# Weights split into a rounded part and a remainder: by two GpSimd DMAs instead of a staging load and a VectorE subtraction

## The chip, the cores and the metric

One core of a Trainium2 chip runs the whole program. The metric is device time in microseconds, from launch to end, as the median of several executions. The engines are TensorE (PE in the profile, with its weight loads as PEld), VectorE (DVE), ScalarE (ACT), GpSimd (POOL) and SyncE (SP, which here only issues DMAs).

## The reference

A two-layer encoder over 512 tokens of width 1024, all in float32. Each layer is a mixer (layer 0: grouped attention and a bidirectional mLSTM; layer 1: neighbourhood attention and differential attention), then cross-attention into 256 memory tokens, then a gated MLP of width 2816 with a convolution over positions. For the change only the matrix products with weights matter:

```python
for l in range(DEPTH):
    h = rms_norm(x, norm_mix[l])
    x = x + mixer(h)                       # h @ w_in ... @ w_out
    x = x + memory_cross_attention(...)    # h @ w_q, m @ w_kv, ... @ w_o
    x = x + conv_ffn(...)                  # h @ w_up, conv, silu(gate) * val, @ w_down
```

## The kernel before

Each product with weights is made in three TensorE passes, so that it comes out near float32. A weight tile W is split into hi, which is W rounded to fp32r (the format in which TensorE takes a 4-byte number at full rate), and lo = W - hi. The activations are split in the same way by earlier code. `mm3` then adds W_hi H_hi, W_hi H_lo and W_lo H_hi in one PSUM bank. So a full weight tile, 128 rows by 1024 columns (512 KB), feeds 8 x 3 = 24 matmuls of 512 columns.

Where a weight tile comes from: `stage` (line 460) loads it from HBM with a DMA on SP's queue into a buffer of class "st". `weights` (line 466) takes a buffer of class "w" (hi in its first 1024 columns, lo in the other 1024) and calls `split` (line 436): a copy with rounding, on ScalarE or VectorE, and then a VectorE subtraction. There are 246 such tiles: 88 for the MLP's up projection, 48 for its down projection (in threes of 1024, 1024 and 768 columns), 24 for the odd mixer's input, 22 for the even mixer's, 32 of 512 columns for the mixers' outputs, 16 for the memory's keys and values, 16 for the query and output projections of cross-attention. One of them, `w1`, is staged by hand at the start of the program.

The order is not the program's text order. `Recorder` records all instructions, `schedule` (line 237) runs a list schedule over them with planned costs (`cost`, line 167), and `trace` emits each engine's instructions in the order that results. On the chip an engine keeps that order and waits in it. Only the order is fixed by the plan, not the times. A buffer of a class is taken at its first write and given back after its last use; the tags boost some instructions, those of weights by 60 places. Of the planned costs these matter here: a matmul is its columns / 2400 + 0.0027; ScalarE needs 0.09 + 0.000835 per column; a step from one engine to another adds `LAT` = 0.13; and of DMAs

```python
            return (0.06 if eng == "sync" else 1.0), 0.0      # line 179: time on the issuing queue
...
                    if e == "gpsimd":
                        end = now + 3.2                       # line 340: planned landing
```

Buffers: 4 of class "st" and 3 of class "w". GpSimd has only 32 `affine_select` (masks of the mLSTM's decay matrices) and some memsets. All recorded instructions are emitted at line 391, so the profile shows them as L391; they are told apart by tile names: st, w, a (activations), p (PSUM), c (columns of statistics), ident.

Of the kernel before, what the change touches and what calls it, by code (L numbers as in the profile page):

```python
# [11 lines left out]
F32 = mybir.dt.float32  # L12
F32R = mybir.dt.float32r
AF = mybir.ActivationFunctionType
OP = mybir.AluOpType
# [7 lines left out]
LN_EXP_SET = 6  # L23
SILU_SET = 18

SLOTS = {"a": (80, 512), "st": (4, 1024), "w": (3, 2048), "c": (48, 8), "p": (8, 512)}

ROWS = "p (i c) -> p i c"
COLS = "p (c i) -> p i c"
# [22 lines left out]


class Buf:
    """A buffer of one slot class; the slot is chosen when the schedule is made."""

    def __init__(self, cls, ap=None):
        self.cls, self.ap = cls, ap
# [1 line left out]


class View:
    """A recorded view of a Buf; resolved to an access pattern when its instruction is traced."""

    def __init__(self, buf, ops, dummy):
        self.buf, self.ops, self.dummy = buf, ops, dummy
# [19 lines left out]
        return View(self.buf, self.ops + (("to_broadcast", shape),), np.broadcast_to(np.int8(0), shape))  # L86

    def grid(self, pattern, i):
        """[p, n] as [p, i, n/i] ("p (i c) -> p i c") or, of columns in the other order, "p (c i) -> p i c"."""
        p, n = self.dummy.shape  # L90
        return View(self.buf, self.ops + (("grid", (pattern, i)),), np.broadcast_to(np.int8(0), (p, i, n // i)))

    def spread(self, n):
        """[p, m] as [p, m, n], each element n times."""
        p, m = self.dummy.shape
        return View(self.buf, self.ops + (("spread", n),), np.broadcast_to(np.int8(0), (p, m, n)))

# [14 lines left out]


class Op:
    """An instruction: alts holds (engine, method, args, keywords, cost, latency) for each engine that may run it."""

    __slots__ = ("idx", "alts", "pick", "preds", "succs", "need", "bufs", "allocs", "end", "placed", "prio", "boost")

# [16 lines left out]


class Recorder:
    """Records instructions with their buffers, orders them by a list schedule, then traces them in that order."""

    LAT = 0.13  # L140

# [93 lines left out]
        return op  # L235

    def schedule(self, slots):
        """List schedule: each engine takes, of the instructions that are ready, the first in program order. A
        buffer is given one of its class's slots with its first write and gives it back after its last use."""
        import heapq  # L240
        n_ops = len(self.ops)
        free = {c: [(0.0, i) for i in range(n)] for c, n in slots.items()}
        room = {c: np.full(n_ops + 1, n) for c, n in slots.items()}
        first, last = {}, {}
# [149 lines left out]
class Kern:  # L394
# [50 lines left out]
            self.nc.scaled(out, src, gain[rows])  # L445

    def rest(self, lo, src, hi, gain=None, rows=slice(None)):
        """lo: what scaled_copy's rounding left of src * gain."""
        if gain is None:
            self.nc.vector.tensor_tensor(lo, src, hi.bitcast(F32), op=OP.subtract)  # L450
        else:
            self.nc.vector.scalar_tensor_tensor(lo, src, gain[rows], hi.bitcast(F32), op0=OP.mult, op1=OP.subtract)
# [11 lines left out]
        return st, w  # L464

    def weights(self, src):
        nc = self.nc
        st, w = src if isinstance(src, tuple) else self.stage(src)
        wb = self._new("w", 2048, F32R)
        wh, wl = wb[:, :1024], wb[:, 1024:]  # L470
        with self.nc.boosted("w"):
            self.split(wh[:, :w], wl[:, :w], st[:, :w])
        return wh, wl

    def gemm(self, out, src, hs, first=True, last=True):
# [35 lines left out]
class Norm:  # L511
# [27 lines left out]
            nc.vector.tensor_tensor(self.acc, self.acc, sq, op=OP.add)  # L539

    def columns(self):
        """rstd, and its square, of token 128 * t + p in row p of columns t and 4 + t."""
        K, nt = self.K, self.n // 128
        nc = K.nc
        p = K.ps("t")[:, :32 * nt]
        for t in range(nt):
            nc.tensor.transpose(p[:, 32 * t:32 * t + 32], self.r[0:32, t * 128:t * 128 + 128], K.ident[0:32, 0:32])
        self.rc = K.col("rc")
        nc.vector.tensor_copy(self.rc[:, :nt].grid(ROWS, nt), p.grid(ROWS, nt)[:, :, 0:1])
        nc.vector.tensor_tensor(self.rc[:, 4:4 + nt], self.rc[:, :nt], self.rc[:, :nt], op=OP.mult)  # L550
# [14 lines left out]


def softmax(K, sc, n, bias=None):
    """exp(sc - max) and 1 / its sum, of sc and of a bias added to it."""
    nc = K.nc
    c = K.col("sm")  # L570
    P = K.a("P")[:, :n]
    if bias is None:
        nc.vector.tensor_reduce(c[:, 0:1], sc, op=OP.max, axis=AX.X, negate=True)
        nc.scalar.activation(P, sc, AF.Exp, bias=c[:, 0:1], accum_out=c[:, 1:2])
    else:
        nc.vector.tensor_tensor_reduce(P, sc, bias, -1.0, 3.0e38, op0=OP.add, op1=OP.min, accum_out=c[:, 0:1])
        nc.scalar.activation(P, P, AF.Exp, bias=c[:, 0:1], scale=-1.0, accum_out=c[:, 1:2])
    nc.vector.reciprocal(c[:, 2:3], c[:, 1:2])
    return P, c[:, 2:3]


class Head:
    """One head, or two (parts) of 64 columns each: score(i, part) -> P of query tile i, finish(Ps) -> P tiles by part,
    v(kt) -> the stationary operands of key block kt by part, take(y)."""

    def __init__(self, score, v, take, finish=None, plan=None, col=None, nkt=4, parts=1):
        self.score, self.v, self.take, self.parts = score, v, take, parts
# [67 lines left out]


def merge(main, fill, name, rest=True):
    """Emit main, with fill's work spread through it (ratio of PE time), and then what is left of fill (rest)."""
    debt, ratio = TUNE[name + "0"], TUNE[name]
    for c in main:  # L660
        debt += c * ratio
        while fill is not None and debt > 0:
            try:
                debt -= next(fill)
            except StopIteration:
                fill = None
        yield c
    if rest and fill is not None:
        yield from fill
# [10 lines left out]


def q_stack(K, q, gain=None):
    """Two heads' [hi; lo] rows: [qa_hi; qa_lo] and [qb_lo; qb_hi]."""
    lo, hi = slice(0, 64), slice(64, 128)
    qa, qb = K.ar("qa"), K.ar("qb")
    for t, src, dst in ((qa, lo, hi), (qb, hi, lo)):
        K.scaled_copy(t[src], q[src], gain, src)
        K.rest(t[dst], q[src], t[src], gain, src)
    return qa, qb


def k_stack(K, k, gain=None):
    """What the stacked q is multiplied with, of two heads: hi against both its halves, lo against its hi half."""
    nc = K.nc
    halves = slice(0, 64), slice(64, 128)
    out = []
    for i, src in enumerate(halves):
        kh, kl = K.ar("kh"), K.ar("kl")
        for dst in halves:
            K.scaled_copy(kh[dst], k[src], gain, src)  # L700
        nc.gpsimd.memset(kl[halves[1 - i]].bitcast(F32), 0.0)
        K.rest(kl[src], k[src], kh[src], gain, src)
        out.append((kh, kl))
    return out


def scores2(K, q2, k2, i, keys=None):
    """Query tile i against all keys, or against two key tiles."""
    nc = K.nc
    p = K.ps("s")  # L710
    c = slice(i * 128, i * 128 + 128)
# [12 lines left out]
def trunk(ctx, tc, xT, memT, vec, lam_in, rope, ev_w, ev_o, od_w, od_o, ca_q, ca_kv, ca_o, up, down, na_u, t5, outT):  # L724
# [19 lines left out]
    nc = K.nc  # L744
# [45 lines left out]
        return t  # L790

    def tok_gemm(w, nrm, width):
        """Token rows times `width` columns of a matrix: a bank holds 512 // width blocks of 128 tokens."""
        kp, per = 1024 // width, 512 // width
        banks = [K.ps("g") for _ in range(nrm.n // (128 * per))]
        chunks = KT // kp
# [14 lines left out]
        return banks  # L811

    class Tok:
        """Token rows: groups of `width` columns, each a list of banks."""

        def __init__(self, width):
            self.width, self.groups = width, []
# [4 lines left out]
            return self.groups[g][b], j * self.width + o  # L822

    def tok_values(w, nrm, v, roll=False):
        """Values, each token row times its rstd; roll: row n goes to row n + 64."""
        width, per = v.width, 512 // v.width
        banks = yield from tok_gemm(w, nrm, width)
        out = [K.a("v") for _ in banks]
# [11 lines left out]
        v.groups.append(out)  # L840

    def tok_norm(w, nrm, width, refine):
        """Token rows, rms_norm over each head of 64, but for its gain. A list of transposed 128-column chunks."""
        per, nh = 512 // width, width // 64
        banks = yield from tok_gemm(w, nrm, width)
        xs = []
# [21 lines left out]
        return xs  # L868

    def tok_heads(w, nrm, width, gain, refine, stack, roll=False):  # L870
        """Heads of 64 with their gain, transposed and stacked; roll: token n goes to column n + 64."""
        per = 512 // width
        xs = yield from tok_norm(w, nrm, width, refine)
        out = []
# [18 lines left out]
        return t  # L893

    def proj_norm(w, m, nrm, ones, gain, n=S, d=64, refine=False):
        """rms_norm over each head of (h * nrm.r) @ w: scale free but for eps, which becomes eps / nrm.r ** 2.
        refine: a Newton step on the root, which turns its sign; gain is negated for it."""
        p = K.ps("g")[:, :n]
        yield from K.gemm(p, w[m], nrm.hs)
        with nc.boosted("qk"):  # L900
            return norm_bank(p, nrm, ones, gain, n, d, refine)
# [277 lines left out]
        yield from odd_proj(nrm, st, 12, TOK["na"], gcol("naq"), vcol("nak"), True)  # L1179

    def na(st, ys):
        """A tile of 128 tokens is 16 grid columns. Keys are turned by 8 columns, so that the windows of query tile i
        lie in key tiles i and i + 1; the last tile's follows on the first, whose halves are at the grid's two ends."""
        def pair(j):
            def score(i, half):
                b = K.a("u")[:, :256]
# [18 lines left out]
    mems = []  # L1205

    def mem_norm(l):
        """The memory times a layer's gain; its rstd is the same for both layers."""
        nm = Norm(K, vcol("mem", 8 * l, 8), 256)
        for k in range(KT):  # L1210
            t = K.a("mem")[:, :256]
# [243 lines left out]


def _rows(yT):
    """The output's columns are tokens in column-major order of the grid."""
    return np.ascontiguousarray(yT.reshape(D, 64, 8).transpose(2, 1, 0)).reshape(1, S, D)


# [13 lines left out]
```

## Time and profile before

| | |
|---|---|
| device time, 3 runs | 1449.54, 1453.91, 1457.04 us |
| median | 1453.91 us |
| span of the profiled execution | 1447.9 us |
| median less that span | 6.0 us |
| TensorE busy | 1430.4 us, 99% of the span |
| VectorE, ScalarE, GpSimd busy | 966.4, 760.4, 24.0 us |
| moved by DMA | 135.70 MB |

The span runs from the first to the last instruction of the profiled execution. The time of that execution by the device's own measure is not listed apart, so the median is put beside the span: 1453.91 - 1447.9 = 6.0 us lie around it. Matmuls are pipelined, so the mean duration of one (390 ns) is longer than the distance from one to the next (about 230 ns).

### The profile page before, as it was taken

What the parts mean: (1) busy time and instruction counts of PE and PEld (TensorE: products, weight loads), DVE (VectorE), ACT (ScalarE), POOL (GpSimd) and SP (SyncE); (2) the same over time, 40 slices, a digit from 0 to 9 for tenths busy, and PEclk for the clock granted to TensorE, in tenths of its full rate; (3) what the DMA queues carried; (4) which work ended last, traced back from release to release, by engine and by line L of the source; (5) the groups of instructions that cost most, each with busy time, mean ns of one, the idle gap of its engine ahead of it and who ended that gap; (6) DMA issues with size and microseconds to landing.
All of it is one profiled execution on the core that took longest, in us unless ns stands there. A gap on an engine that the chain in (4) does not pass through costs nothing. (4 is left out here: it accounts for less than half of the span.)

```text
span 1447.9 us, 17456 instructions
## 1 busy us (share of the span) xinstructions
PE 1430.4 (99%) x6463; PEld 1130.6 (78%) x6463; DVE 966.4 (67%) x1744; ACT 760.4 (53%) x1334; POOL 24.0 (2%) x60
## 2 busy tenths in 40 slices
PE   8999999999999999999999999999999999999998
PEld 5787777786888888888888767877778888888887
DVE  7885587666867776733458797857568777776221
ACT  6575697667444444422346777866754444443111
POOL 0000011000000000000000000000000000000000
PEclk9999999999999999999999999999999999999999
DMA  6221221231232333333252402433213332322421
GB/s 235 73 73 59 66 80 56 79 118 45 88 101 90 100 90 100 88 95 97 86 197 67 138 30 88 154 95 107 76 58 90 100 96 94 99 91 66 142 95 48
DMA packets 48182, 135.70 MB, mean 94 GB/s; under 512 B 5473, under 2 KB 12129, under 8 KB 48097
## 3 DMA queue, kind: packets, MB, share of 16 engines
q1 hardware_dynamic: 48096, 134.60, 29.3%
q8 instruction: 50, 0.82, 0.2%
q14 instruction: 36, 0.29, 0.1%
HBM read 132.48 MB, written 2.10 MB: 93 GB/s over the span
## 5 line engine op out<-in xcount | busy, mean ns | idle before, releaser
L391 PE MATMUL p<-a,w 128*128 128x512 f32 (+1 forms) x4560 | 1067.8, 390 | 0.5 <-DVE w L391 0.5
L391 PEld LDWEIGHTS p<-a,w 128*128 128x128 f32 x4560 | 840.7, 188 | 198.1 <-issue 14.6
L391 DVE TENSOR_TENSOR w<-st,w 128x1024 fp32r<-128x1024 f32 (+2 forms) x246 | 279.3, 1136 | 160.7 <-ACT w L391 160.0
L391 ACT CAST w<-st 128x1024 fp32r<-128x1024 f32 (+2 forms) x219 | 213.6, 977 | 247.9 <-PE p L391 221.8
L391 PE MATMUL p<-w,a 128*128 128x512 f32 x768 | 202.2, 402 | 0.9 <-DVE w L391 0.6
L391 DVE SCALAR_TENSOR_TENSOR a<-a,vec,a 128x504 f32<-128x504 f32 (+3 forms) x324 | 183.3, 590 | 11.6 <-ACT a L391 7.5
L391 DVE TENSOR_TENSOR a<-a,a 128x512 fp32r<-128x512 f32 (+5 forms) x215 | 143.4, 670 | 37.5 <-ACT a L391 34.2
L391 PEld LDWEIGHTS p<-w,a 128*128 128x128 f32 x768 | 140.8, 188 | 35.3 <-issue 5.9
L391 DVE TENSOR_TENSOR a<-p,a 128x512 f32<-128x512 f32 (+2 forms) x127 | 85.4, 673 | 108.3 <-PE p L391 82.2
L391 ACT ACTIVATE a<-a 128x512 f32<-128x512 f32 (+2 forms) x170 | 100.7, 600 | 102.3 <-DVE a L391 101.1
L391 PE MATMUL p<-a,a 128*128 128x512 f32 (+1 forms) x424 | 135.0, 432 | 6.6 <-ACT a L391 5.6
L391 ACT CAST a<-a 128x512 fp32r<-128x512 f32 (+2 forms) x92 | 55.9, 608 | 149.3 <-DVE a L391 148.4
L391 ACT ACTIVATE a<-a,vec 128x512 f32<-128x512 f32 (+2 forms) x139 | 105.8, 764 | 43.0 <-DVE a L391 41.4
L391 ACT ACTIVATE a<-a,c 128x256 f32<-128x256 f32 (+3 forms) x172 | 98.4, 598 | 19.6 <-DVE c L391 19.2
L391 PEld LDWEIGHTS p<-a,a 128*128 128x128 f32 x424 | 76.3, 191 | 31.9 <-ACT a L391 10.0
L391 DVE TENSOR_TENSOR a<-a,p 128x512 f32<-128x512 f32 (+1 forms) x65 | 47.9, 738 | 58.4 <-PE p L391 58.4
L391 PEld LDWEIGHTS p<-ident,a 128*128 128x128 f32 (+2 forms) x474 | 55.5, 140 | 26.4 <-DVE a L391 7.3
L391 PE MATMUL p<-ident,a 128*128 128x128 f32 (+2 forms) x474 | 70.0, 273 | 4.2 <-DVE a L391 3.5
L391 ACT COPY a<-p 128x512 f32<-128x512 f32 (+1 forms) x121 | 61.0, 536 | 18.0 <-PE p L391 17.6
L391 ACT ACTIVATE a<-p,c 128x512 f32<-128x512 f32 (+2 forms) x81 | 48.3, 609 | 24.8 <-DVE c L391 17.0
L391 DVE TENSOR_REDUCE c<-p 128x1 f32<-128x512 f32 (+1 forms) x64 | 34.5, 553 | 13.7 <-PE p L391 12.7
L391 ACT ACTIVATE a<-p 128x512 f32<-128x512 f32 (+1 forms) x58 | 30.9, 533 | 20.3 <-PE p L391 20.1
(73 smaller groups left out, 483.3 us busy)
## 6 DMA issues: line engine op xcount, KB each, us to landing
st<-in_up_dram SPq DMA_DIRECT2D x88, 512.0 KB, 3.5
st<-in_down_dram SPq DMA_DIRECT2D x32, 512.0 KB, 3.6
st<-in_od_w_dram SPq DMA_DIRECT2D x24, 512.0 KB, 4.2
st<-in_ev_w_dram SPq DMA_DIRECT2D x22, 512.0 KB, 3.6
st<-in_ca_kv_dram SPq DMA_DIRECT2D x16, 512.0 KB, 4.4
st<-in_down_dram SPq DMA_DIRECT2D x16, 384.0 KB, 3.2
st<-in_ev_o_dram SPq DMA_DIRECT2D x16, 256.0 KB, 2.5
st<-in_ca_q_dram SPq DMA_DIRECT2D x8, 512.0 KB, 3.5
```

The source lines that it names most:

```text
L391: getattr(getattr(nc, eng), fn)(*[r(v) for v in args], **{k: r(v) for k, v in kw.items()})
```

## The change

The tiles that come by `weights` are no longer staged. A DMA on GpSimd's queue reads the tile from HBM and writes it, cast to fp32r, into the hi half of its "w" buffer. ScalarE writes -hi into the lo half. A second DMA on GpSimd's queue reads the same tile from HBM again and adds it onto what lies in the lo half. The VectorE subtraction and the copy (which could run on either engine) are gone for them. The tile `w1`, staged by hand, is split as before. There are now 4 "w" buffers and 1 "st" buffer, and no planned cost is changed. The rest of the diff takes out docstrings.

```diff
-SLOTS = {"a": (80, 512), "st": (4, 1024), "w": (3, 2048), "c": (48, 8), "p": (8, 512)}
+SLOTS = {"a": (80, 512), "st": (1, 1024), "w": (4, 2048), "c": (48, 8), "p": (8, 512)}
...
     def weights(self, src):
+
         nc = self.nc
-        st, w = src if isinstance(src, tuple) else self.stage(src)
         wb = self._new("w", 2048, F32R)
         wh, wl = wb[:, :1024], wb[:, 1024:]
+        if isinstance(src, tuple):
+            st, w = src
+            with self.nc.boosted("w"):
+                self.split(wh[:, :w], wl[:, :w], st[:, :w])
+            return wh, wl
+        w = src.shape[1]
         with self.nc.boosted("w"):
-            self.split(wh[:, :w], wl[:, :w], st[:, :w])
+            nc.gpsimd.dma_start(wh[:, :w], src)
+            nc.scalar.activation(wl[:, :w], wh[:, :w].bitcast(F32), AF.Copy, scale=-1.0)
+            nc.gpsimd.dma_start(wl[:, :w], src, accum_op=OP.add)
         return wh, wl
```

## Rows read from the trace of the kernel before

**Rows 1.** The page's head: span, busy time of each engine, instructions.

```profile
span 1447.9 us, 17456 instructions
PE 1430.4 (99%) x6463; PEld 1130.6 (78%) x6463; DVE 966.4 (67%) x1744; ACT 760.4 (53%) x1334; POOL 24.0 (2%) x60
```

**Rows 2.** Waits of PE: engine, tile <- releaser: us in total, times, longest.

```profile
PE p L391 <- ACT a L391: 6.3, 4, 5.6
PE p L391 <- DVE a L391: 5.7, 9, 1.0
PE p L391 <- DVE w L391: 1.1, 2, 0.6
```

**Rows 3.** Groups by line: busy us, mean ns, idle before and its releaser.

```profile
L391 DVE TENSOR_TENSOR w<-st,w 128x1024 fp32r<-128x1024 f32 (+2 forms) x246 | 279.3, 1136 | 160.7 <-ACT w L391 160.0
L391 DVE CAST w<-st 128x1024 fp32r<-128x1024 f32 (+2 forms) x27 | 18.0, 665 | 13.9 <-PE p L391 13.9
```

**Rows 4.** Windows: PE, PEld, DVE, ACT, POOL busy (instructions), PEclk, DMA share, GB/s.

```profile
0.00:5.60 5.60, 0.00 (x0) 0.00 (x0) 1.65 (x7) 2.62 (x3) 3.61 (x12) 1.00 0.51 163
5.60:14.00 8.40, 8.31 (x25) 4.97 (x25) 6.47 (x12) 6.46 (x9) 0.00 (x0) 1.00 1.04 374
150.00:250.00 100.00, 100.00 (x520) 74.31 (x519) 75.94 (x199) 82.49 (x172) 15.16 (x38) 1.00 0.22 71
345.00:588.00 243.00, 243.00 (x1053) 197.07 (x1052) 176.26 (x225) 109.19 (x140) 0.00 (x0) 1.00 0.30 93
```

**Rows 5.** Windows of VectorE's work on tile w: busy us (instructions), PEclk, DMA share, GB/s.

```profile
0.00:50.00 50.00, 10.47 (x9) 1.00 0.55 187
100.00:150.00 50.00, 13.37 (x14) 1.00 0.18 53
400.00:588.00 188.00, 41.68 (x34) 1.00 0.31 95
588.00:705.00 117.00, 26.96 (x24) 1.00 0.31 92
705.00:775.00 70.00, 14.37 (x12) 1.00 0.42 140
775.00:870.00 95.00, 14.70 (x13) 1.00 0.24 79
870.00:920.00 50.00, 10.89 (x11) 1.00 0.38 124
```

**Rows 6.** DMA issues: count, KB each, median us from issue to landing.

```profile
st<-in_up_dram SPq DMA_DIRECT2D x88, 512.0 KB, 3.5
st<-in_ev_o_dram SPq DMA_DIRECT2D x16, 256.0 KB, 2.5
a<-in_t_dram SPq DMA_DIRECT2D x16, 256.0 KB, 5.8
```

**Rows 7.** The DMA queue of SP: packets, MB, share of 16 engines' span.

```profile
q1 hardware_dynamic: 48096, 134.60, 29.3%
```

**Rows 8.** Tile st in the up projection (345 to 588): duration ns min/median/max, first and last start.

```profile
L391 ACT CAST w<-st x41: 1037/1052/1056, 349.9 to 583.3; 128x1024 fp32r<-128x1024 f32 x41
L391 SPq DMA_DIRECT2D st<-in_up_dram x41: 327/328/328, 352.3 to 574.5; - x41
```

**Rows 9.** Timeline, 12 to 15: start us, us, instruction [idle before <-releaser].

```profile
12.85 1.05 ACT L391 CAST w<-st 128x1024 fp32r<-128x1024 f32 x1 [0.56 <-DMA st<-in_ev_w_dram]
...
13.93 1.23 DVE L391 TENSOR_TENSOR w<-st,w 128x1024 fp32r<-128x1024 f32 x1 [0.33 <-ACT w L391]
```

**Rows 10.** GpSimd's own work by groups.

```profile
L391 POOL TENSOR_SCALAR_AFFINE_SELECT a<-a 128x128 f32<-128x128 f32 x32 | 12.0, 383 | 59.4 <-ACT a L391 47.2 <-PE p L391 11.2 <-POOL a L391 0.5
L391 POOL MEMSET a<- 64x512 f32 (+1 forms) x22 | 11.2, 519 | 725.8 <-DVE a L391 454.1 <-PE p L389 161.7 <-PE p L391 109.6
```

## The prediction

> **What bounds the kernel now.** I read the page's head first: TensorE is busy for 1430.4 of 1447.9 us, and no other engine comes above 67% [rows 1]. Then who TensorE waits for. Of the 17.5 us that it is not busy, 5.6 us lie ahead of the first matmul [rows 4], and its named waits come to 13 us, of which only 1.1 us are for a weight tile [rows 2]. Then the stages by windows. Through the up projection TensorE is busy for all of 243 us at a granted clock of 1.00, with VectorE at 176 and ScalarE at 109 us [rows 4]. A tile there lasts 188 / 34 = 5.53 us, counted by VectorE's subtractions [rows 5]. The reader is to see that VectorE and ScalarE have room in the stages that hold most tiles, so what is taken off them there gives nothing back. What a change to the weights can do is make TensorE wait, if a tile takes longer than 5.53 us to come.
>
> **What goes.** 246 subtractions and 27 VectorE casts, 297 us of VectorE [rows 3], less one pair for `w1`. They lie under TensorE's work, so I cost them at nothing. The most they could return is the 12 us for which TensorE waited for activations from ScalarE and VectorE [rows 2]. SP loses 245 DMAs of 0.33 us [rows 8]. ScalarE keeps one pass over each tile, the negation instead of the cast; no row shows it, and the cast of the same size, 1.05 us [rows 8], is the nearest. The 27 tiles that VectorE cast add 27 us to ScalarE's 760, under cover.
>
> **What comes: a chain in one queue.** GpSimd issues two DMAs for each tile, 490 in all, in a fixed order, and the second cannot be issued before ScalarE has negated what the first brought. What stands behind it in the queue waits too, and that is mostly the first DMA of the next tile. So the order decides, and it follows from the planner's costs. In the up projection a buffer comes free every 24 x 0.216 = 5.18 planned us, and then the hi DMA is issued. Its lo DMA is ready 3.2 + 0.13 + 0.945 + 0.13 = 4.41 later, before the next buffer is free. So the queue reads hi, lo, hi, lo, and four buffers do not help: the next hi stands behind a lo that waits. The tile's cycle c on the chip is the hi's landing, the negation, and the issue of the lo with the next hi right behind it.
>
> **The size of c.** A 256 KB tile lands 2.5 us after its issue and one of 512 KB after 3.5 us, each alone on the queue [rows 6]: by the two, 2.0 us for 512 KB and 1.5 us that do not depend on size. With transfers back to back a tile is cheaper: 134.60 MB took 29.3% of the span, 424 us, so 317 GB/s or 1.65 us for 512 KB [rows 7]. That a transfer waits for those ahead of it shows in the 256 KB tiles of the T5 bias, 5.8 us instead of 2.5 [rows 6]. The hi of the next tile follows the lo in the same queue, so it waits for the lo's transfer. What an accumulating transfer takes no row shows. Bound below: as much as a plain one, 1.65 us. Bound above: three times the slower price, 6.0 us, for reading the weight, reading the lo half and writing it, one after the other. I take twice 1.65 = 3.3 us, since it reads two operands of 512 KB where a plain one reads one. What GpSimd needs to issue a DMA no row shows either: below, nothing beyond SP's 0.33 us [rows 8], which the landing times contain; above, twice its 0.52 us memset [rows 10], 1.0 us. I take the lower, since the issue can run while the transfer ahead is moving. The hand-over from ScalarE to its successor is 13.93 - 12.85 - 1.05 = 0.03 us [rows 9]; 0.1 us for two. So
>
> c = 1.5 + 3.3 + 1.65 + 1.05 + 0.1 = 7.6 us.
>
> With an accumulate as cheap as a plain transfer c = 5.95. If the hi did not wait for the lo at all, c = 3.5 + 1.05 + 0.1 + 0.33 = 5.0. With all upper bounds c = 1.5 + 6.0 + 2.0 + 1.15 + 1.0 = 11.65.
>
> The Trainium skill (DMA: Bandwidth & Descriptors, section "Latency and other measured facts") gives about 1 us to the first byte for DMAs issued from GpSimd, against 0.6 us for those from SP. No run here shows a GpSimd DMA yet; by that rule c would be 8.0 us and the sum below 68 us larger.
>
> **The sum, stage by stage**, at c = 7.6 against the time that a tile has now:
>
> - Up projections: 88 tiles x (7.6 - 5.53) = 182 us.
> - Down projections: 16 groups of three tiles; three last 117 / 8 = 14.6 us now [rows 5]. The third has 18 matmuls, 3.89 planned us, so the hi behind it is issued before the lo of the tile ahead and one wait in three goes: 2c + 1.65 = 16.85, so 16 x 2.25 = 36 us.
> - Odd mixer's input before attention joins in: 12 tiles, 70 / 12 = 5.83 us each [rows 5]: 12 x 1.77 = 21 us.
> - Query and output projections of cross-attention, 16 tiles, 24 matmuls each, so 5.53 us: 16 x 2.07 = 33 us.
> - Start: 9 tiles in the first 50 us [rows 5], 9 x 2.07 = 19 us. Until 14 us the DMA engines are full, 1.04 at 374 GB/s [rows 4], with the loads of x. SP's queue no longer holds weights back behind x, and several hi DMAs of 0.52 MB may now start at once; I add 3 us, about two of them at that rate.
> - Short tiles between 100 and 150 us and between 870 and 920 us, mostly keys and values of the memory: 14 and 11 tiles, 3.6 and 4.5 us each [rows 5]. There hi's and lo's interleave, and the DMA engines' own 3 x 1.65 = 4.95 us per tile is the limit: 14 x 1.35 + 11 x 0.45 = 24 us.
> - Attention mixed with tiles, 775 to 870 us: 13 tiles at 7.3 us [rows 5]: 4 us. The other attention stages have longer intervals; nothing.
> - The mLSTM: GpSimd's 32 `affine_select` [rows 10] now stand in the queue behind lo DMAs that wait. A hi lands 1.5 + 3.3 + 1.65 = 6.45 us after its turn where the plan has 3.2, so each of some 8 tiles can hold a mask for 3 us; half of it under TensorE's other work, 12 us.
>
> Together 182 + 36 + 21 + 33 + 22 + 24 + 4 + 12 = 334 us. The span becomes 1447.9 + 334 = 1782 us, and with the 6.0 us by which the median lies above the span, 1788 us. One microsecond of c is worth 88 + 32 + 12 + 16 + 9 + 13 = 170 us.
>
> The Trainium skill (Collectives: The Full Stack, section "The bandwidth ceiling: the fold count and why AG ≠ RS ≠ AR") says that a reduction in the DMA engines runs at half the rate of a copy, since it emits two reads per chunk. No row here shows it; it would give the factor of two that I took.
>
> **The rivals.**
>
> *Hidden.* The hi does not wait for the lo, or the queue's order leaves two tiles in flight, and c stays under 5.53 us. For it: c = 5.0 at the lowest bounds; three buffers ahead of the one in use are 16.6 us of TensorE's work; the DMA engines are busy for only 0.30 of the up projection [rows 4], and two transfers per tile, 4.95 us, still fit in 5.53. Against it: 0.5 us of margin, eaten by any one of the prices above. Result: 1454 us and a few more from the start, no change.
>
> *Faster.* The mechanism is VectorE's 297 us: in the attention stages TensorE's 12 us of waits for ScalarE and VectorE go away [rows 2]. Result: 1454 - 12 = 1442 us. It decides only if c stays under 5.53, so it is a part of the case before.
>
> *Cheap accumulate.* c = 5.95: the sum shrinks to 37 us in the up projections and about 23 elsewhere, 1514 us. It lies at the range's low end.
>
> *The DMA engines are the limit.* If an accumulate costs three times 2.0 us and GpSimd's issue comes on top, c = 11.65, and 334 + 4.05 x 170 = 1020 us are lost: about 2475 us. For it: nothing bounds the accumulate. Against it: no transfer of this size in the trace takes near 6 us alone.
>
> *The clock falls.* TensorE would stand for 2 us of each 7.6. In every window read the granted clock is 1.00 [rows 4, 5], so no row shows a fall. At the lower of its two levels, 1.2 GHz, a tile would take 11 us and hide the chain; the up projections alone would lose 88 x 5.5 = 484 us, the other dense stages in proportion (334 / 182) about 400 more: some 2340 us.
>
> **How the numbers follow.** Hidden 0.11, faster 0.05, slower 0.84: of it 0.09 for the cheap accumulate, 0.71 for c between that and 9.4, 0.02 for the DMA engines as the limit, 0.02 for the clock. Slower, same and faster are meant by 0.5%, 7 us, about what three runs that spread over 7.5 us can tell. The predicted time is that of the likeliest case, 1788 us. The range begins at 1500 us, under the cheap accumulate, and ends at 2100 us, where c is 9.4; what it leaves out is hidden and faster, 0.16, and the last two rivals, 0.04. The chain's own range, without the cheap accumulate, is 1560 to 2060 us.
>
> **What would show it.** Right: TensorE's busy share falls to near 81%, its idle time is put down to DMAs into w, and in the up projection the tile's interval is near 7.6 us and the waits of GpSimd's queue are for ScalarE's write of w. The lo DMA's landing minus that of a hi tells the accumulate's price. The odd one out should be the attention stages, with intervals nearly unchanged. Wrong: an interval of 5.53 us in the up projection (hidden), hi DMAs issued in pairs ahead of a lo (the order I derived fails), GpSimd's queue waiting for nothing while DMA engines are at 1.0 (they are the limit), or a granted clock below 1.00.

## The result, and the profile after

The change made the kernel slower: 1690.91 us median (1688.73 to 1692.79, 4 runs) against 1451.72 us for the kernel before on the same chip, ratio 1.164 with a 95% interval of [1.162, 1.167]. Forecast were 1788 us and a range of 1500 to 2100 us: the sign held, the time lies inside the range, and the loss was 239 us where 334 were summed.

The page of the changed kernel, its head and GpSimd's DMA queue (packets, MB, share of 16 engines' span):

```profile
span 1687.6 us, 17569 instructions
PE 1502.9 (89%) x6463; PEld 1151.8 (68%) x6463; DVE 720.2 (43%) x1536; ACT 744.7 (44%) x1297; POOL 371.7 (22%) x550
...
q0 software_dynamic: 70560, 235.96, 62.7%
```

Against [rows 1] VectorE has lost 246 us of work, and TensorE stands for 185 us instead of 17.5. No engine and no queue is full: GpSimd's transfers occupy the DMA engines for 62.7% of the span, GpSimd itself is busy for 22%. So the time went into waits (engine, tile <- releaser: us, times, longest):

```profile
POOL w L391 <- ACT w L391: 955.7, 210, 9.9
...
PE p L391 <- DMA w<-in_up_dram: 49.3, 38, 3.7
PE p L391 <- DMA w<-in_down_dram: 47.1, 30, 3.7
```

GpSimd's queue waited 955.7 us for ScalarE's writes of w, at 210 of 245 tiles, and TensorE now waits for weights, which in [rows 2] cost it 1.1 us. The timeline of GpSimd in the second up projection shows the chain itself (start, us, DMAs issued, [wait before them]); below it ScalarE's negations in the same stretch:

```profile
1343.70 0.88 POOL L391 DMA_DIRECT2D w<-in_up_dram  x1 [7.08 <-ACT w L391]
1345.36 1.42 POOL L391 DMA_DIRECT2D w<-in_up_dram  x2 [0.78 <-ACT w L391]
1354.60 1.45 POOL L391 DMA_DIRECT2D w<-in_up_dram  x2 [7.83 <-ACT w L391]
1362.63 1.96 POOL L391 DMA_DIRECT2D w<-in_up_dram  x3 [6.59 <-ACT w L391]
1370.72 0.88 POOL L391 DMA_DIRECT2D w<-in_up_dram  x1 [6.12 <-ACT w L391]
```

```profile
1353.24 1.06 ACT L391 ACTIVATE w<-w 128x1024 fp32r<-128x1024 f32 x1 [5.85 <-DMA w<-in_up_dram]
...
1361.28 1.06 ACT L391 ACTIVATE w<-w 128x1024 fp32r<-128x1024 f32 x1 [3.72 <-DMA w<-in_up_dram]
```

Read it from 1354.60: lo of one tile and hi of the next are issued in 1.45 us (x2). The hi lands and releases ScalarE at 1361.28, 6.68 us after the lo's issue. The negation takes 1.06 us, and at 1362.63 the next lo goes out: a cycle of 8.03 us. From 1343.70 to 1370.72 four tiles (eight DMAs) take 27.02 us, 6.75 us each, where TensorE needs 5.53 [rows 5].

Where the time went, stage by stage, is marked by ScalarE's loads of activation tables, which the program makes at the start of each MLP and after its up projection (after, then before):

```profile
413.83 1.28 ACT L382 ACT_TABLE_LOAD   x1
679.50 1.28 ACT L382 ACT_TABLE_LOAD   x1
1244.19 1.28 ACT L382 ACT_TABLE_LOAD   x1
```

```profile
376.16 1.28 ACT L382 ACT_TABLE_LOAD   x1
609.97 1.28 ACT L382 ACT_TABLE_LOAD   x1
1088.49 1.28 ACT L382 ACT_TABLE_LOAD   x1
```

The last column adds up the prediction's terms that fall into each stage.

| stage, from mark to mark | before | after | more | forecast |
|---|---|---|---|---|
| even mixer, cross-attention | 376.2 | 413.8 | 37.7 | 69.5 |
| up projection, layer 0 | 233.8 | 265.7 | 31.9 | 91 |
| down projection, odd mixer, cross-attention | 478.5 | 564.7 | 86.2 | 64.5 |
| up and down projection, layer 1 | 359.4 | 443.4 | 84.0 | 109 |
| sum | 1447.9 | 1687.6 | 239.7 | 334 |

### The profile page after: what moved, and what is told of

Read it like the earlier page. It is cut to its first block, busy times and chain, and to the rows that moved or that the text cites. A ratio compares the mean times of both kernels' runs of the same rounds, so it can differ in the third digit from the quotient of the medians.

```text
span 1687.6 us, 17569 instructions
## 1 busy us (share of the span) xinstructions
PE 1502.9 (89%) x6463; PEld 1151.8 (68%) x6463; DVE 720.2 (43%) x1536; ACT 744.7 (44%) x1297; POOL 371.7 (22%) x550
## 3 DMA queue, kind: packets, MB, share of 16 engines
q0 software_dynamic: 70560, 235.96, 62.7%
## 5 line engine op out<-in xcount | busy, mean ns | idle before, releaser
L391 PE MATMUL p<-a,w 128*128 128x512 f32 (+1 forms) x4560 | 1122.3, 400 | 113.3 <-DMA w<-in_up_dram 49.3
L391 PEld LDWEIGHTS p<-a,w 128*128 128x128 f32 x4560 | 856.6, 193 | 348.5 <-DMA w<-in_up_dram 67.1
L391 ACT ACTIVATE w<-w 128x1024 fp32r<-128x1024 f32 (+2 forms) x245 | 241.7, 986 | 653.5 <-DMA w<-in_down_dram 216.1
L391 POOL DMA_DIRECT2D w<-in_up_dram x176 | 124.9, 858 | 499.1 <-ACT w L391 443.6
L391 PE MATMUL p<-w,a 128*128 128x512 f32 x768 | 213.7, 416 | 10.8 <-DVE a L391 3.2
L391 DVE TENSOR_TENSOR a<-a,a 128x512 fp32r<-128x512 f32 (+4 forms) x215 | 143.7, 671 | 98.7 <-ACT a L391 95.0
L391 PE MATMUL p<-a,a 128*128 128x512 f32 (+1 forms) x424 | 138.1, 435 | 14.9 <-DVE a L391 8.6
L391 POOL DMA_DIRECT2D w<-in_down_dram x96 | 68.8, 863 | 243.5 <-ACT w L391 233.4
L391 ACT ACTIVATE a<-a,vec 128x512 f32<-128x512 f32 (+2 forms) x127 | 96.2, 761 | 18.8 <-DVE a L391 18.7
L391 ACT ACTIVATE a<-a,c 128x256 f32<-128x256 f32 (+2 forms) x153 | 88.7, 598 | 16.2 <-DVE c L391 15.5
L391 POOL DMA_DIRECT2D w<-in_od_w_dram x48 | 34.3, 774 | 161.0 <-ACT w L391 73.5
L391 POOL DMA_DIRECT2D w<-in_ev_w_dram x42 | 29.9, 736 | 128.9 <-ACT w L391 79.1
```

Source lines behind the costliest of these rows:

```text
L391: getattr(getattr(nc, eng), fn)(*[r(v) for v in args], **{k: r(v) for k, v in kw.items()})
```

## The experiments

The theory on trial is the *chain*: a tile's lo DMA waits for ScalarE, and through the queue's order the next tile's hi waits behind it. Its rivals are *transfer* (the DMA engines cannot move both transfers in a tile's time) and *issue* (GpSimd needs too long to issue).

**1. The prices by themselves.** A kernel of weight loads alone: one at a time, eight back to back, and a cast behind an accumulate.

> A kernel that only moves weight tiles of 512 KB: six of each kind one at a time (a plain load from SyncE's queue, a casting load from GpSimd's queue, an accumulating one from GpSimd's queue), eight of each kind back to back, and six times an accumulate with a cast right behind it. It computes nothing of the reference. Chain theory (the second DMA of a tile waits for ScalarE, and the next tile's first DMA stands behind it in GpSimd's queue): alone, plain 3.5 us from issue to landing, cast about 4, accumulate about 5.5; back to back 1.65 us for each plain or cast, about 3.0 for each accumulate; the cast behind an accumulate lands 6.5 to 7.5 us after the accumulate's issue. Transfer theory (the DMA engines cannot move two transfers of a tile in the 5.53 us that TensorE needs for it): accumulates back to back 4 us or more each.

Its DMA issues (count, KB, median us to landing), ScalarE's reads of two of the eight accumulates as they land, and the eight casts back to back (issue: duration ns, first and last start us; then us to landing):

```profile
one_plain<-in_up_dram SPq DMA_DIRECT2D x6, 512.0 KB, 3.3
one_cast<-in_up_dram POOLq DMA_DIRECT2D x6, 512.0 KB, 3.6
one_accum<-in_up_dram POOLq DMA_DIRECT2D x6, 512.0 KB, 5.3
pair_hi<-in_up_dram POOLq DMA_DIRECT2D x6, 512.0 KB, 5.9
```

```profile
166.29 1.06 ACT L776 ACTIVATE zero<-run_accum 128x1024 f32<-128x1024 f32 x1 [1.41 <-DMA run_accum<-in_up_dram]
168.76 1.06 ACT L776 ACTIVATE zero<-run_accum 128x1024 f32<-128x1024 f32 x1 [1.41 <-DMA run_accum<-in_up_dram]
```

```profile
L747 POOL DMA_DIRECT2D run_cast<-in_up_dram x8: 527/527/554, 139.3 to 145.9; - x8
DMA to landing us min/median/max: 3.6/5.9/7.0
```

Alone an accumulate takes 1.7 us more than a cast. Back to back one lands every 2.47 us, less than the 3.3 taken. The casts back to back land from 142.9 to 152.9 us, 1.4 us each; after the first gap of 2.3 us the landings in the trace lie 1.28 us apart (median), and so do those of the eight plain loads. So the 1.65 us read from [rows 7] was too much for a plain or a casting load. The hi behind a lo is issued 0.95 us after it and lands 5.9 us later, 6.85 us behind the lo's issue; 6.45 had been summed. The Trainium skill (Collectives: The Full Stack, "The bandwidth ceiling: the fold count and why AG ≠ RS ≠ AR") gives a reduction between cores half the rate of a copy, since it reads two sources. Back to back the trace agrees: 2.47 / 1.28 = 1.9.

**2. The order alone.** One planner's number, so that the plan issues the next hi ahead of a lo:

```diff
-                        end = now + 3.2
+                        end = now + 6.0
```

> The changed kernel with one planner's number changed: a GpSimd DMA is planned to land 6.0 us after its issue instead of 3.2, so that the plan issues the next tile's first DMA ahead of the second DMA of the tile before. Same instructions, same transfers, other order. Chain theory: every wait of GpSimd's queue for ScalarE is covered by a tile's time; the up projection falls from 6.75 to 5.5 to 5.7 us per tile and the whole to 1460 to 1510 us. Transfer theory: the same bytes through the same engines, 1690 us within 1%. Issue theory (GpSimd's 1.4 us of issuing per tile): also 1690 us.

1504.17 us, ratio 1.036 [1.033, 1.038]. Same instructions and bytes, 187 us faster than the changed kernel. A window of its second up projection (busy us of PE, PEld, DVE, ACT, POOL; PEclk, DMA share, GB/s):

```profile
1150.00:1290.00 140.00, 140.00 (x609) 113.96 (x608) 79.37 (x152) 61.00 (x77) 35.53 (x51) 1.00 0.86 191
```

TensorE is busy for all of it, 609 matmuls or 25.4 tiles, 5.5 us each, and the DMA engines, at 0.86, carry two transfers per tile without holding anything up. The transfer and issue theories fall with this run: what each tile moves and issues is unchanged.

**3. The one wait, taken away, and its control.** hi and lo get buffers of their own, and the negation reads zeros instead of hi, but is planned as if it read hi; the control keeps the true negation:

```diff
-            nc.scalar.activation(wl[:, :w], wh[:, :w].bitcast(F32), AF.Copy, scale=-1.0)
+            nc.hold = nc.ops[-1]
+            nc.scalar.activation(wl[:, :w], self.zero[:, :w], AF.Copy, scale=-1.0)
+            nc.hold = None
```

> The changed kernel with hi and lo in buffers of their own, the order of a plan in which the negation still follows the first DMA, but the negation reads a tile of zeros, so that on the chip it and the second DMA need not wait for the first one's landing. The lo half then holds the weight itself and not the remainder. Same number of DMAs, negations and accumulates. Chain theory: the wait is gone, 1460 to 1510 us. Transfer theory: unchanged, 1690 us. Clock theory (TensorE loses by a lower clock): in between only as far as TensorE has gaps.

> The changed kernel with hi and lo in buffers of their own, and nothing else changed: the control for the run in which the negation no longer needs the first DMA, with the same order of instructions as that run. Chain theory: as the changed kernel, 1690 us within 3%, so that the whole difference to that run's 1478 us is the one wait. If separate buffers alone bring the time under 1550 us, that run proves nothing about the wait.

1478.41 us, 1.017 [1.014, 1.019], and for the control 1737.88 us, 1.197 [1.193, 1.200]. In one order of instructions, with all transfers kept, the wait for the hi's landing is worth 259 us. In the profiled execution of the control TensorE stands for 217 us where it stands for 37 without the wait, and is busy for 81 us longer, at a mean granted clock of 0.960 against 0.997.

**4. The accumulate as a plain load.**

```diff
-            nc.gpsimd.dma_start(wl[:, :w], src, accum_op=OP.add)
+            nc.gpsimd.dma_start(wl[:, :w], src)
```

> The changed kernel with the second DMA as a plain casting load that overwrites the lo half instead of accumulating onto it; it still waits for ScalarE, and the order is the same. The lo half then holds the weight itself. Chain theory: the transfer that a first DMA waits behind is shorter by about 1.4 us, three times in four tiles: 27.0 - 4.2 = 22.8 us for four tiles in the up projection, 5.7 each, and 1490 to 1530 us in all. Transfer theory: 3.3 us of transfer per tile, no longer a limit, 1455 us. Issue theory: unchanged, 1690 us.

1496.78 us, 1.031 [1.028, 1.033]. The shorter transfer ahead of each hi pulls the cycle under TensorE's time: behind one lo it is 6.64 us (1217.34 to 1223.98) instead of 8.03, and between 1150 and 1290 us TensorE is busy for all 140 us, 5.5 us per tile and not the 5.7 expected. So in this order of the queue the accumulate's extra transfer decides whether the chain binds there; run 2 hides the full accumulate by another order.

**5. ScalarE's step doubled.** Each negation is emitted twice, in the unchanged order.

```diff
+            if fn == "activation" and args[2] == AF.Copy and kw.get("scale") == -1.0:
+                nc.scalar.activation(*[r(v) for v in args], **{k: r(v) for k, v in kw.items()})
             getattr(getattr(nc, eng), fn)(*...)
```

> The changed kernel with each negation made twice by ScalarE, in the same order of instructions on every engine. Chain theory: each wait of GpSimd's queue for ScalarE becomes 1.0 us longer; there are three in four tiles of the second up projection and about two in three elsewhere, so some 160 in the dense stages: 100 to 180 us more, 1790 to 1870 us. Transfer theory and issue theory: ScalarE was busy for 44% only, no change, 1690 us within 1%.

1882.20 us, 1.296 [1.293, 1.300], 191 us above the changed kernel, 12 over the upper end. 242 us of extra work went onto an engine that was busy for 44%, and 191 us more came out at the end. Some of them are a slower TensorE, at a mean clock of 0.933 and busy for 73 us longer than in the changed kernel. In the second up projection four tiles now take 30.45 us (1456.13 to 1486.58): three waits, each 1.1 us longer.

**6. hi by DMA alone.** SyncE stages the weight, VectorE subtracts, GpSimd's DMA makes hi; 4 "st" and 3 "w" buffers.

```diff
             nc.gpsimd.dma_start(wh[:, :w], src)
-            nc.scalar.activation(wl[:, :w], wh[:, :w].bitcast(F32), AF.Copy, scale=-1.0)
-            nc.gpsimd.dma_start(wl[:, :w], src, accum_op=OP.add)
+            st, _ = self.stage(src)
+            nc.vector.tensor_tensor(wl[:, :w], st[:, :w], wh[:, :w].bitcast(F32), op=OP.subtract)
```

> One half of the change alone: hi comes by GpSimd's casting DMA, the weight is also staged by SyncE's queue, and VectorE subtracts as in the kernel before, with that kernel's buffers (4 staging, 3 of hi and lo). No negation, no accumulate, the weights are read from HBM twice. Chain theory: no DMA waits for another, so the time of the kernel before, 1450 to 1470 us, a little more only at the start, where more transfers meet. Transfer theory: two plain transfers, 3.3 us per tile, under 5.53: also no change. If casting DMAs from GpSimd cost something by themselves, it shows here as over 1480 us.

1483.92 us, 1.023 [1.019, 1.026], a miss: 32 us over the kernel before, with no chain of DMAs, and above the 1480 us that were to tell of a cost of the casting DMAs themselves. By the table loads the MLPs take what they took (234.0 us for the first up projection, 359.7 us for the last stage); the first mixer with its cross-attention takes 14.9 us more, the second with the down projection 18.7. TensorE stands for 38.5 us instead of 17.5, but only 3.1 us of its waits are for weights (1.1 before [rows 2]). The largest group is

```profile
PE p L391 <- ACT a L391: 18.3, 13, 7.5
```

Why ScalarE's activations come later, by the transfers or by the other order that this version's plan has, is not shown.

**7. The start.** As run 2, with GpSimd's first weight DMA held behind the last tile of x.

```diff
+    nc.gpsimd.tensor_copy(K.col("gate"), x[7][:, :8])
+    K.gate = nc.ops[-1]
...
+            nc.hold = self.gate
             nc.gpsimd.dma_start(wh[:, :w], src)
+            nc.hold = None
```

> The run with a planned landing of 6.0 us (1504 us), and in addition GpSimd's first weight DMA waits until the last tile of x has landed. Chain theory with the start as a cost of its own (weights and x share the DMA engines): TensorE gets back some 8 to 12 us of the first 100 us, 1490 to 1498 us. If the start is not what is left, 1504 us.

1509.55 us, 1.040 [1.037, 1.043]: no gain over run 2's 1504.17. TensorE's first 24 matmuls run nearly in one piece again, yet in the first 100 us it does 337 operations against 342 in run 2. So the meeting of weights and x is not what is left, as far as one gate can show.

**8. Other orders.** A planned landing of 4.5 us, and a planner that is told 2.47 us from run 1 for a lo and, for a hi, the 1.65 us of [rows 7], where run 1 gives 1.28:

```diff
-                        end = now + 3.2
+                        part, acc = _free(args[1]) / 1024, "accum_op" in o.pick[3]
+                        t_dma = max(t_dma, now + cost) + part * (2.47 if acc else 1.65)
+                        end = t_dma + (1.85 if acc else 0.95)
```

> As the run with a planned landing of 6.0 us, but 4.5. In the up projections each hi is again issued one tile ahead. Chain theory: no wait in the dense stages, and 1480 to 1510 us, a little better or worse than 1504 us by what the mixers make of the order. Transfer theory: 1690 us.

> The changed kernel with the planner told the prices measured by themselves: transfers of 1.65 us (hi) and 2.47 us (lo) for 512 KB one after the other on one set of engines, landing 0.95 and 1.85 us later. In the up projections its order is hi, hi, lo, lo for pairs of tiles. Chain theory: one long wait per pair, as in the changed kernel's first up projection, 6.3 us per tile in both, and 1570 to 1630 us in all. If true prices in the plan were enough, 1470 to 1500 us.

1515.84 us, 1.044 [1.042, 1.047], 6 us over the upper end, though TensorE is busy throughout in both up projections (430 to 630 and 1160 to 1300 us), and 1538.38 us, 1.060 [1.057, 1.062], better than expected. The order hi, hi, lo, lo of the second plan hides the chain in the second up projection after all (between 1200 and 1300 us TensorE is busy throughout). There ScalarE starts a pair's two negations 2.7 us apart (1202.42 and 1205.12). In the changed kernel's first up projection, with the same order of DMAs, they start 4.0 us apart (465.85 and 469.82), since ScalarE first waits for VectorE with another operation. That the gap makes the difference is argued, not tested. 79 of the 90 us that this version's span is longer than that of the kernel before lie in the two stages with the mixers.

**9. Is the rest the price of another order?** Two small changes to the plan of the kernel before, `LAT` 0.13 to 0.17, and `flex` 0.54 to 0.45.

> The kernel before, with one planner's number changed: a step from one engine to another is planned at 0.17 us instead of 0.13. Same instructions, another order. It is for the 23 to 52 us that are left in every version in which the chain is gone, nearly all in the mixers. If what is left is the price of an order that does not fit as well as the old one, 1465 to 1490 us here too. If it is a cost of GpSimd's DMAs (shared DMA engines, late bias tiles), this kernel, which has none, stays within 0.5% of 1452 us.

> The kernel before, with another planner's number changed: VectorE's handicap for work that two engines can do is 0.45 instead of 0.54. As for the run above: 1465 to 1490 us if the old order is a narrow optimum, within 0.5% of 1452 us if what is left is a cost of GpSimd's DMAs.

1454.79 us, 1.002 [1.001, 1.003], and 1452.98 us, 1.001 [1.000, 1.002]. By these two the old kernel's order is no narrow optimum. That the 26 to 52 us that runs 2, 3 and 6 keep come with GpSimd's DMAs is then likely, but not shown: these two runs move other instructions, and among the versions with GpSimd's DMAs the order alone makes 1504, 1516 or 1538 us (runs 2 and 8).

No version beat the kernel before, whose TensorE was busy for 99% [rows 1].

## Why the prediction was right, and where its sizes were off

*What bounds the kernel.* Right. VectorE's 246 us came back as nothing, and in no run does TensorE go under 5.5 us per tile in the up projection. They are 246 and not 297 us because the planner gave VectorE 64 operations more of other kinds (1744 - 273 = 1471 before, 1536 - 1 = 1535 after). They came from ScalarE, which was busy for 744.7 us and not for the 787 summed.

*The chain.* Right, and shown three ways: another order hides it (run 2, 187 us less), cutting the one wait removes 259 us (run 3), lengthening it costs 191 us (run 5). Yet of the prediction's own four signs of being wrong two came in part, hi DMAs in pairs ahead of a lo and a clock below 1.00: the mechanism held, the order and the clock did not.

*"So the queue reads hi, lo, hi, lo."* This is the step that was off. I took ScalarE and GpSimd as free in the plan, and a lo ready at 4.41 of 5.18 planned us. The order of the program has, in the first up projection (number among GpSimd's 490 DMAs, tile, source),

```
140 DMA w_3092 <-in_up_dram     hi
141 DMA w_3122 <-in_up_dram     hi
142 DMA w_3092 <-in_up_dram     lo
143 DMA w_3122 <-in_up_dram     lo
```

for every pair of tiles from the sixth tile on, and in the second one such pair in four tiles. The plan's own times say why. A buffer comes free at 415.80 planned us, but GpSimd is planned to be issuing a lo until 416.32, so the first hi goes out 0.52 us late. The next buffer comes free at 420.98, 4.66 us after that hi and not 5.18. ScalarE has begun a copy of 0.52 us at 419.59, just before it could have begun the negation, so this lo is ready at 421.18, and at 420.98 the next tile's hi goes first. The prediction left out the 1.0 us that the plan takes for each issue on GpSimd, and ScalarE's other work. So the up projections lost 31.9 and about 44 x (6.75 - 5.53) = 54 us, 86 together, where 182 were summed. That is as much as the 95 us by which the sum was too high, by luck: the other errors below, about 32 us too much at the start, 29 too little in the down projections and 8 in the odd mixer's stage, nearly cancel.

*c = 7.6 us.* 8.03 us behind one lo: landing 6.68 instead of 6.45, negation 1.06 as taken from the cast, hand-over 1362.63 - 1361.28 - 1.06 = 0.29 instead of 0.1. That the landing came out so near is luck in part: by run 1 the accumulate is 2.47 us and not 3.3 (its factor of two held, the 1.65 was too large) and the hi behind it 1.28 and not 1.65, so that 6.68 - 2.47 - 1.28 = 2.9 us are left where the sum had 1.5. Behind two lo's, which the sum did not have, the cycle is 9.24 us (1345.36 to 1354.60).

*Down projections.* Forecast 16.85 us for three tiles, measured 18.65 (1572.47 to 1591.12), since one hi in three follows two accumulates: 16 x (18.65 - 14.6) = 65 us instead of 36.

*Start, short tiles, masks.* The first stage lost 37.7 us where 69.5 were summed, the odd mixer's stage about 86.2 - 32 = 54 without its down projection where 46.5 were. These terms were not taken apart by a run.

*The rivals.* Hidden and faster did not occur: the margin of 0.5 us that I gave it was missing. The DMA engines were no limit (run 2). The clock did fall, which no row of before had shown, but in short stretches, where that rival had it low throughout. It fell where the chain leaves gaps in TensorE's work, though not after each of them: of the gaps of 3.13 us before 831.52 and 3.78 us before 839.27 only the second has a fall near it in these windows of 10 us (the columns of [rows 4]):

```profile
830.00:840.00 10.00, 4.70 (x19) 3.42 (x20) 2.04 (x3) 3.87 (x5) 2.28 (x3) 1.00 1.08 378
840.00:850.00 10.00, 6.42 (x18) 4.49 (x18) 0.33 (x2) 2.26 (x3) 1.42 (x2) 0.67 0.83 191
```

After a stretch with TensorE busy for 4.70 of 10 us the mean is 0.67: part of the window is at the lower of the two levels, 1.2 GHz (0.5). In the second up projection one tile in four is slowed as well: the 24 matmuls at 1367.98, behind a gap of 1.77 us, take 7.39 us from the first's start to the last's end, where the 24 at 1341.02 take 5.83. Four tiles of 5.53 us and 1.56 more are 23.7 us, under the chain's 27, so there the clock costs nothing. Over the span the mean is 0.973, so 5.4% of it, 91 us, at half speed: at most 46 us of work lost. TensorE's busy time rose by 72.5 us for the same 6463 operations. Part of the rest is an estimate from two numbers: TensorE stops 117 times more often than before, and at each stop the last matmul's record of 390 ns is not overlapped by a next one 230 ns later, 117 x 0.16 = 19 us. The share is 89% where 81% was forecast: the span, shorter than forecast, makes it 85% (1430.4 of 1687.6 us), and the longer busy time the rest. How much of the slower clock reached the end in the mixers was not measured. With the chain gone the mean is 0.991 (run 2), 0.997 (runs 3 and 6).

*Open.* What the 26 to 52 us are that stay, mostly in the stages with the mixers, without the chain. Two changes of the plan cost the old kernel next to nothing (run 9), a gate on the start gained nothing (run 7), and run 6 has no accumulate. The traces name waits, but not one cause. In run 3 TensorE stands for 37.4 us instead of 17.5, and 28.9 us of its waits are for DMAs of weights, the largest group of them

```profile
PE p L391 <- DMA w<-in_ev_w_dram: 8.6, 2, 6.8
```

In run 6 it waits for other results of ScalarE and VectorE, 30.3 us against 12.2 in the kernel before, and hardly for weights. In run 2 the lower clock can hold up to 13 us of it, half of 1.8% of 1501 us; in runs 3 and 6, at 0.997, no more than 5.

## What to carry to other kernels

Here a DMA that waited in GpSimd's queue held every DMA behind it. So for a load in two steps (load, compute, accumulate) try an order with the next tile's first step ahead of this tile's second; here that one reordering was worth 187 us with the same instructions. Before believing an order derived by hand, list the queue's order, and count the planned time of the queue itself. The 246 us taken here from an engine that was not the bound returned nothing.

## What the hardware showed

An accumulating DMA of 512 KB issued from GpSimd lands after 5.3 us alone, a casting one after 3.6, a plain one from SyncE after 3.3. Back to back an accumulate lands every 2.47 us and a cast or a plain load every 1.28 (run 1). Issuing takes GpSimd 0.86 us for an accumulate and 0.55 for a cast, more than SyncE's 0.33 [rows 8]. The Trainium skill (DMA: Bandwidth & Descriptors, "Latency and other measured facts") has 0.4 us between the first bytes of DMAs issued from GpSimd and from SP; the plain and casting loads here differ by 0.3 from issue to landing.
